# Token rows fetched ahead into the weight-staging pool, transposed tiles requested a step earlier, and seven attention output tiles, in a hybrid attention and linear-attention step

## The chip, the cores and the metric

The kernel runs on one core of a Trainium2 chip. The core has a matrix engine (PE, with its weight loads shown apart as PEld), a vector engine (DVE), an activation engine (ACT), a general engine (POOL), and a sequencer (SP) that in this kernel issues every DMA. Sixteen DMA engines carry the transfers. Each engine works through its own queue in order and waits there for semaphores. The metric is the device time of one execution in microseconds; lower is better.

## What is computed

One step of a one-layer decoder: 2048 prompt tokens, and 8 sequences with 8 new tokens each ("sample"), model width 1024, all in float32 at the interface. Cut to what matters:

```python
h = rmsnorm(x, norm_w)
z = h @ w_in                                   # 1024 x 3600
q, k, v, qb, kb, vb, g_lr, gate_a, gate_b = jnp.split(z, split_points(), axis=-1)
q = rope(rmsnorm(heads(q, 8), q_norm_w), pos)
k = rope(rmsnorm(heads(k, 8), k_norm_w), pos)
o_a = attend(q, k, heads(v, 8))                # three dilated windows, mixed by their denominators
log_a = log_sigmoid(g_lr @ w_gate_up + b_gate) / 16
o_b, s_fin = gla_chunked(qb * 64**-0.5, kb, vb, log_a, s0)
o_b = rmsnorm(o_b, gla_norm_w)
mixed = concat([o_a * silu(gate_a), o_b * silu(gate_b)])
y = x + mixed @ w_out
```

The attention has three branches: (window, dilation) = (128, 1), (512, 4) and (2048, 16). In a branch with dilation d the tokens of one residue modulo d form a sequence of their own, and each query sees 129 keys of it at most. The branch results are combined per token and head with weights from their maxima and softmax denominators.

## The kernel before

**Numbers in two halves.** Every float32 operand of a large product is split into two float16 parts (high and low). A projection of 128 tokens is 24 matrix products: 8 blocks of 128 inputs, and high x high, high x low, low x high.

**Normalised tokens.** `fetch(t)` (L464) loads the row block of 128 tokens `x_t`; `prep(t)` (L474) normalises it: a square with a sum on ACT into the scratch tile `jk` (L487), a reciprocal root in six small steps on ACT and DVE, a scaled copy on ACT (L495) and a difference on DVE (L496) into the two halves `ht`, then one transposing DMA `ht` to `hl` (L499) and a store of `hl` (L503) for later stages. The first four row blocks use two tiles of another pool (tag `qq`); those from 4 on and the sample's share a single buffer, tag `x` of pool `xp`. `ht` has one buffer as well. `hl` has four.

**Weights.** `load_w` (L544) loads a block of `w_in` as eight raw pieces of 128 rows (L554) into the pool `wr`, which has eight buffers of 128 x 528 float32; it finds a scale and splits them into `w` (L603, L604). Three such blocks are held at a time.

**First stage.** `first(m)` (L1085 on) runs over groups of four token tiles. Group 0 projects v, q and k of tiles 0 to 3; behind each k projection tile t+4 is fetched and prepared. Groups 1 to 3 project v, q, k of each tile and prepare tile t+4 up to tile 15. The results go through DRAM: the two-part `qp_d`, `kp_d`, `vp_d`. Behind `first(m)` the attention units of branches 1 and 2 of group m are put in a queue, and are worked off in small steps (`pump`) during the projections of group m+1.

**Attention.** `attend` (L395) makes an item of four steps: `pre` loads; `qk` makes scores in a PSUM bank and, on DVE, adds the mask and finds the row limit (L416), then takes the exponential on ACT (L419), whose sums go to the output tile; `tr` transposes the probabilities on PE and splits them; `pv` multiplies with the values, and `post` joins the halves (`added`, L458) into the output tile and stores it (L847, L903). Several items are in flight: two score banks, three score tiles `s`, three probability tiles `pt`.
- Branches 1 and 2: a unit is four heads of one block of 128 queries, in two items of two heads. Its output tile `o` (4 heads x 66 columns) is one of four in pool `op`. The transposed queries `qq` of a group and half come by four transposing DMAs (L801) in `queries`, are then exchanged between the partition halves by two DVE copies (`exchanged`, L794), and have two buffers.
- Branch 3: 16 residues with all eight heads, in two items (even heads, odd heads). Transposed queries and keys `T_q` and `T_k` (L883), two buffers each, the exchange (L794) right behind them, values `v` (L890), and one output tile of eight heads with two buffers, stored after the second item (L903).

**Beside and behind it.** During groups 2 and 3 and branch 3, POOL and DVE form the sample's dot products with the cached keys (L928, L929), whose loads are the most numerous DMAs. The projections qkb, g and vb run beside branch 3. Then come the linear attention (beside the rest of g, vb and gb), the combination of the branches and the output projection (L1431).

**Order.** The program is traced in the order of the code; a scheduler then orders each engine's instructions with a time model of its own. An instruction may stand far from its place in the code, as far as its data and its buffers allow, but the order on each queue is fixed once the kernel is compiled.

Of the kernel before, what the change touches and what calls it, by code (L numbers as in the profile page):

```python
# [18 lines left out]
P = 128  # L19
D = 1024  # L20
# [32 lines left out]
def tile_hymba(ctx: ExitStack, tc: tile.TileContext, A: dict):  # L53
# [292 lines left out]
    with ExitStack() as c1:  # L346
# [12 lines left out]

        wr = right(c_in, "wr", 8)  # L360
        zp = right(c_in, "zp", 2)
# [6 lines left out]
        ptp = c_att.enter_context(tc.tile_pool(name="ptp", bufs=3))  # L368
        op = c_att.enter_context(tc.tile_pool(name="op", bufs=4))
        ap_ = c_att.enter_context(tc.tile_pool(name="ap", bufs=2))  # L370
# [93 lines left out]
        def fetch(t):  # L464
            n = NS if t == "s" else P
            if t in (0, 1, 2, 3):
                if t % 2 == 0:
                    early.append(ap_.tile([P, 2, D], F32, name=f"x_{t}", tag="qq"))
                x = xs[t] = early[-1][:, t % 2]
            else:  # L470
                x = xs[t] = xp.tile([P, D], F32, name=f"x_{t}", tag="x", bufs=1)
            SP.dma_start(x[:n], x_s if t == "s" else x_p[t * P : (t + 1) * P, :])

        def prep(t):  # L474
            again[0] += 1
            n = NS if t == "s" else P
            u = again[0]
            x = xs.pop(t)[:]
            if t == "s":
# [7 lines left out]
            ACT.activation(jk[:n], x[:n], AF.Square, accum_out=ss[:n])  # L487
            rs = sm.tile([P, 1], F32, name=f"rs_{u}", tag="rs")
            rsqrt(sm, rs[:n], ss[:n], 1.0 / D, n, 1, f"x{u}", H_SCALE)
            if t != "s":  # L490
                if t < 4:
                    ht = early_ht[:, t]
                else:
                    ht = xp.tile([P, 2, D], F16, name=f"ht_{u}", tag="ht", bufs=1)[:]
                ACT.activation(ht[:, 0], x, AF.Copy, scale=rs[:])  # L495
                DVE.scalar_tensor_tensor(  # L496
                    ht[:, 1], x, rs[:], ht[:, 0], ALU.mult, ALU.subtract
                )
# [45 lines left out]
        def load_w(name, between=(), behind=()):  # L544
# [7 lines left out]
            for k in range(KT):  # L552
                raw = wr.tile([P, 528], F32, name=f"wr_{name}_{k}", tag="wr")
                SP.dma_start(raw[:, :n], src[k * P : (k + 1) * P, c0 : c0 + n])  # L554
# [241 lines left out]
        def queries(m, pp):  # L796

            q = qs_[m, pp] = ap_.tile([P, 2, 4, 512], F16, name=f"qq_{m}_{pp}", tag="qq")
            for a in range(4):
# [3 lines left out]
                )  # L803
            exchanged(*(q[:, a].rearrange("p h c -> p (h c)") for a in (1, 0)))

        def unit(m, pp, br, x):
# [13 lines left out]
            def pre():  # L820
                if (br, x) == (1, 0):
                    if pp == 0:
                        for a in range(4):
                            keys(m, a)
                        yield
                    queries(m, pp)
                    yield
# [47 lines left out]


        def branch3(r):
            T = {}

            def pre():  # L880
                for nm_, src, nb in (("q", qp_d, 16), ("k", kp_d, 8)):
                    t = b3.tile([P, nb, P], F16, name=f"T3_{nm_}_{r}", tag=f"T{nm_}")
                    SP.dma_start_transpose(t[:, 0:8], by16(src, r))  # L883
                    T[nm_] = t
                exchanged(
                    *(T["q"][:, a : a + 8].rearrange("p h i -> p (h i)") for a in (8, 0))
                )
                yield
                T["v"] = b3.tile([P, 1024], F16, name=f"v3_{r}", tag="v3")
                SP.dma_start(T["v"][:], by16(vp_d[:], r))  # L890
                T["o"] = b3.tile([P, NH, 66], F32, name=f"o3_{r}", tag="o3")

# [5 lines left out]
            def post(a):  # L898
                added(
                    T["o"][:].rearrange("p (i a) d -> p i a d", a=2)[:, :, a, 0:64], T["O", a][:]  # L900
                )
                if a:
                    SP.dma_start(by16(o3_d[:], r), T["o"][:].rearrange("p h d -> p (h d)"))  # L903

# [3 lines left out]
                    lambda i, a=a: [  # L908
                        (T["q"][:, 8 * part + 2 * i + a], T["k"][:, 2 * i + a])
                        for part in range(2)  # L910
                    ],
                    m3,
                    lambda i, b, a=a: T["v"][:, (2 * i + a) * P : (2 * i + a + 1) * P],
                    lambda i, a=a: T["o"][:, 2 * i + a, 65:66],
                    lambda i, a=a: T["o"][:, 2 * i + a, 64:65],
                    lambda i, a=a: OT(a, i),
# [914 lines left out]
```

## Time and profile before

| What | Value |
|---|---|
| Three runs | 1472.43, 1477.07, 1477.95 us; median 1477.07 |
| Profiled execution | 1483.62 us, span 1481.8 us |
| PE, share of the span | 1272.1 us, 86% |
| DVE | 1007.6 us, 68% |
| ACT | 855.7 us, 58% |
| POOL | 623.7 us, 42% |
| Granted TensorE clock, mean | 0.949 |

"Busy" is the time in which an engine executes; matrix products overlap, so a busy PE is not a PE at its peak. A row of waits names an engine and line that stood idle, who released it, and the total, the count and the longest. "DMA a<-b" is a transfer, from its issue to its landing. "SPq" is SP issuing or waiting. A chain of waits follows the last instruction back to what released each step.

By stage, in time: the first projections of group 0 (to about 95 us), the rest of them and the start of group 1 (to 170), groups 1 to 3 with branches 1 and 2 (to 676), branch 3 (to 853), linear attention (to about 1190), output.

### The profile page before, as it was taken

The numbers are of one execution on the slowest core, as the hardware profiler recorded it, in microseconds if no ns is written. First come the engines' busy times: TensorE is split into PE (matmuls) and PEld (weight loads), VectorE is DVE, ScalarE is ACT, GpSimd is POOL, SyncE is SP. The second block draws the span as 40 slices with busy tenths as digits, with TensorE's granted clock in tenths as the row PEclk, the third lists the DMA queues.
The fourth block names the chain that finished last, engine by engine and source line by source line (L and its number), as shares of the span: only waits on it lengthen the run. The fifth ranks groups of instructions, "written<-read, shape, count | busy, mean of one in ns | idle before, by whom it ended". The sixth has DMA issues, their size and how long they took to land.

```text
span 1481.8 us, 26480 instructions
## 1 busy us (share of the span) xinstructions
PE 1272.1 (86%) x8878; PEld 738.0 (50%) x8878; DVE 1007.6 (68%) x2444; ACT 855.7 (58%) x2295; POOL 623.7 (42%) x565
## 2 busy tenths in 40 slices
PE   3884997888888778887689999898988979989997
PEld 1332554555555545555457756566655535444343
DVE  6384878788887846766756535798988598783222
ACT  6443686676657756766667844687786553231110
POOL 0051424566656535554431167555553155541000
PEclk9897999999999989999799999999999989999999
DMA  9765665678756599878877553343234569998662
GB/s 277 217 168 173 178 193 138 167 213 212 205 153 173 148 229 265 285 203 220 217 186 177 150 152 101 83 137 124 92 102 158 177 239 337 361 304 287 221 204 73
DMA packets 254810, 285.36 MB, mean 193 GB/s; under 512 B 125825, under 2 KB 156626, under 8 KB 254674
## 3 DMA queue, kind: packets, MB, share of 16 engines
q1 hardware_dynamic: 254674, 283.67, 65.3%
q8 instruction: 70, 1.15, 0.3%
q14 instruction: 66, 0.54, 0.1%
HBM read 183.19 MB, written 75.24 MB: 174 GB/s over the span
## 4 chain that ended last, share of the span: by engine, by line
PE 26%; DVE 26%; DMA 25%; ACT 11%; issue 6%; POOL 3%; SPq 3%; DVEq 0%; POOLq 0%; ACTq 0%
PE Y L1431 7%; DMA qb<-q_d 4%; DMA o_d<-o 4%; PE acc_vb L1065 3%; PE OS L1680 3%; DVE p L416 3%; ACT p L419 2%; DMA T_q<-qp_d 2%; PE acc_g L1065 2%; DMA x<-in_x_prompt 2%; DMA k<-in_cache_k_win 2%; POOL pr L928 2%; DVE qbd L220 1%; DVE sck L929 1%; ACT E L209 1%
## 5 line engine op out<-in xcount | busy, mean ns | idle before, releaser
L928 POOL TENSOR_TENSOR pr<-k,qb 128x512 f32<-128x512 f32 x128 | 172.3, 1346 | 205.9 <-DVE sck L929 121.5
L1065 PEld LDWEIGHTS <-hr 128*128 128x128 f16 x1824 | 178.1, 100 | 142.5 <-issue 27.6
L419 ACT ACTIVATE p<-p,o 128x256 f32<-128x256 f32 (+1 forms) x384 | 173.1, 453 | 129.2 <-DVE o L416 110.2
L1065 PEld LDWEIGHTS <-hl 128*128 128x128 f16 x1248 | 124.0, 101 | 178.4 <-issue 52.0
L1431 PE MATMUL Y<-w_o,mh 128*128 128x512 f16 x768 | 181.5, 383 | 8.4 <-ACT mh L1397 5.0
L441 PE MATMUL O<-v,pt 128*128 128x128 f16 x1200 | 119.0, 225 | 48.5 <-POOL pt L393 18.1
L393 POOL TENSOR_TENSOR pt<-p,pt 128x512 f16<-128x512 f32 (+1 forms) x80 | 92.8, 1159 | 147.6 <-ACT pt L392 126.7
L426 PE MATMUL t<-ident,p 128*128 128x128 f32 x600 | 121.1, 296 | 18.1 <-ACT p L419 16.2
L929 DVE TENSOR_REDUCE sck<-pr 128x8 f32<-128x512 f32 x128 | 87.2, 681 | 58.7 <-POOL pr L928 58.5
L441 PEld LDWEIGHTS <-pt 128*128 128x128 f16 x1200 | 86.1, 101 | 79.8 <-POOL pt L393 24.5
L1431 PEld LDWEIGHTS <-mh 128*128 128x128 f16 x768 | 72.1, 98 | 102.9 <-issue 23.2
L1065 PE MATMUL acc_v<-w_v,hl 128*128 128x512 f16 x384 | 96.6, 400 | 25.6 <-ACT zs_q L648 11.0
L416 DVE CUSTOM_DVE_ANT_0 p<-s,m3w,scl_s 128x128 f32<-128x128 f32 (+1 forms) x256 | 88.6, 395 | 30.3 <-DMA o_d<-o 26.5
L408 PE MATMUL s<-kk,qq 128*128 128x256 f16 (+1 forms) x512 | 81.6, 277 | 26.4 <-DVE o L416 25.1
L1065 PE MATMUL acc_g<-w_g,hr 128*128 128x272 f16 (+1 forms) x768 | 103.2, 283 | 1.0 <-ACT vbs L722 1.0
L1065 PE MATMUL acc_q<-w_q,hl 128*128 128x512 f16 x384 | 95.5, 395 | 6.5 <-DVE vp L735 6.5
L1065 PE MATMUL acc_vb<-w_vb,hr 128*128 128x512 f16 x384 | 94.1, 392 | 2.8 <-DVE so_g L622 2.8
L1065 PE MATMUL acc_k<-w_k,hl 128*128 128x512 f16 x384 | 92.0, 383 | 3.9 <-ACT zs_k L648 3.4
L426 PEld LDWEIGHTS t<-ident,p 128*128 128x128 f32 x600 | 74.3, 149 | 40.2 <-ACT p L419 29.2
L1397 ACT ACTIVATE mh<-tm 128x1024 f16<-128x1024 f16 x32 | 31.7, 1020 | 104.9 <-PE tm L1396 98.6
L1065 PE MATMUL acc_gb<-w_gb,hr 128*128 128x512 f16 x384 | 89.8, 388 | 2.1 <-DVE so_gb L622 2.1
L209 ACT ACTIVATE E<-D_e 128x256 f32<-128x256 f32 (+1 forms) x168 | 67.9, 412 | 27.6 <-DVE ks L216 19.1
(526 smaller groups left out, 2685.5 us busy)
## 6 DMA issues: line engine op xcount, KB each, us to landing
k<-in_cache_k_win SPq DMA_DIRECT2D x104, 256.0 KB
sv<-in_cache_v_win SPq DMA_DIRECT2D x104, 256.0 KB
hr<-h_d SPq DMA_DIRECT2D x44, 512.0 KB
qb<-q_d SPq DMA_DIRECT2D x64, 256.0 KB
oc<-o_d SPq DMA_DIRECT2D x48, 264.0 KB
o_d<-o SPq DMA_DIRECT2D x64, 132.0 KB
x<-in_x_prompt SPq DMA_DIRECT2D x16, 512.0 KB
h_d<-hl SPq DMA_DIRECT2D x16, 512.0 KB
```

The costliest lines, as they stand in the source:

```text
L209: ACT.activation(E[rows, i, :n], D[rows, half], AF.Exp, scale=1.0 / 16.0)
L393: POOL.tensor_tensor(l, f, h, ALU.subtract)
L408: PE.matmul(s_ps[:, i * w : (i + 1) * w], q, k, start=(n == 0), stop=(n == len(prods) - 1),)
L416: DVE.tensor_tensor_reduce(s[:, sl], s_ps[:, sl], mask, neg, BIG, ALU.add, ALU.min, nmf(i))
L419: ACT.activation(s[:, sl], s[:, sl], AF.Exp, bias=nmf(i), scale=-1.0, accum_out=denf(i))
L426: PE.transpose(p_ps[:, i * P : (i + 1) * P], t["s"][:, i * P : (i + 1) * P], ident[:])
L441: PE.matmul(o_, t["pt"][:, c, (i * nb + b) * P : (i * nb + b + 1) * P], vf(i, b), start=(n == 0), stop=(n == 2 * nb - 1),)
L928: POOL.tensor_tensor(pr[:], kt, qt, ALU.mult)
L929: DVE.tensor_reduce(out, pr[:].rearrange("p (u k d) -> p u k d", u=2, k=4), AX.X, ALU.add)
L1065: PE.matmul(z, a_[:, k, :], w[:, p_, k, cols], start=(k == 0 and i == 0), stop=(k == KT - 1 and i == 2),)
L1431: PE.matmul(Y[:], a_[:, k, :], w_[:, part, k, :512], start=(i == 0), stop=(i == len(prods) - 1),)
L1680: PE.matmul(OS[32 * x : 32 * x + 32, 0:256], ps(x), vs_[bb][:, 256 * u : 256 * u + 256], start=(i == 0), stop=(i == 13),)
```

## The change

Token rows from tile 4 on move out of their single buffer into the raw-weight pool, whose buffers become four pairs of raw pieces; a row block takes one pair, each of its halves 512 of 528 columns. `load_w("k")` is followed by fetches of tiles 4, 5 and 6; behind the k projection of tile t, and in groups 1 and 2, the fetch is that of tile t+7 (preparation stays at t+4). The sample's rows use the `ht` buffer. The transposed queries of a group's first half are requested at the end of `first(m)`, those of the second half in the unit (branch 2, residue 1) of the first half; the exchange is made where a half's units begin. In branch 3 the T tiles of residue r+1 are requested ahead of residue r's exchange; the heads of an item are 4a to 4a+3 instead of every second one; and each item has an output tile of its own from the pool `op`, which now has seven, with a store of its own.

```diff
-        wr = right(c_in, "wr", 8)
+        wr = right(c_in, "wr", 4)
-        op = c_att.enter_context(tc.tile_pool(name="op", bufs=4))
+        op = c_att.enter_context(tc.tile_pool(name="op", bufs=7))
...
+            elif t == "s":
+                x = xs[t] = xp.tile([P, D], F32, name=f"x_{t}", tag="ht", bufs=1)
             else:
-                x = xs[t] = xp.tile([P, D], F32, name=f"x_{t}", tag="x", bufs=1)
+                x = wr.tile([P, 2, 528], F32, name=f"x_{t}", tag="wr")[:, :, :512]
+                xs[t] = x
+                SP.dma_start(x, x_p[t * P : (t + 1) * P, :].rearrange("p (a c) -> p a c", a=2))
+                return
...
-                raw = wr.tile([P, 528], F32, name=f"wr_{name}_{k}", tag="wr")
+                if k % 2 == 0:
+                    pair = wr.tile([P, 2, 528], F32, name=f"wr_{name}_{k}", tag="wr")
+                raw = pair[:, k % 2]
...
-            exchanged(*(q[:, a].rearrange("p h c -> p (h c)") for a in (1, 0)))
...
-                    queries(m, pp)
+                    q = qs_[m, pp]
+                    exchanged(*(q[:, a].rearrange("p h c -> p (h c)") for a in (1, 0)))
+                    yield
+                elif (pp, br, x) == (0, 2, 1):
+                    queries(m, 1)
                     yield
...
+        def turned3(r):
+            for nm_, src, nb in (("q", qp_d, 16), ("k", kp_d, 8)):
+                t = b3.tile([P, nb, P], F16, name=f"T3_{nm_}_{r}", tag=f"T{nm_}")
+                SP.dma_start_transpose(t[:, 0:8], by16(src, r))
+                T3[r][nm_] = t
...
             def pre():
-                for nm_, src, nb in (("q", qp_d, 16), ("k", kp_d, 8)):
-                    t = b3.tile([P, nb, P], F16, name=f"T3_{nm_}_{r}", tag=f"T{nm_}")
-                    SP.dma_start_transpose(t[:, 0:8], by16(src, r))
-                    T[nm_] = t
+                if r == 0:
+                    turned3(0)
+                if r < 15:
+                    turned3(r + 1)
+                yield
                 exchanged(
                     *(T["q"][:, a : a + 8].rearrange("p h i -> p (h i)") for a in (8, 0))
                 )
-                yield
...
-                T["o"] = b3.tile([P, NH, 66], F32, name=f"o3_{r}", tag="o3")
+                for a in range(2):
+                    T["o", a] = op.tile([P, 4, 66], F32, name=f"o3_{r}_{a}", tag="o")
...
             def post(a):
-                added(
-                    T["o"][:].rearrange("p (i a) d -> p i a d", a=2)[:, :, a, 0:64], T["O", a][:]
-                )
-                if a:
-                    SP.dma_start(by16(o3_d[:], r), T["o"][:].rearrange("p h d -> p (h d)"))
+                o = T["o", a]
+                added(o[:, :, 0:64], T["O", a][:])
+                SP.dma_start(
+                    by16(o3_d[:, 264 * a : 264 * a + 264], r), o[:].rearrange("p h d -> p (h d)")
+                )
...
-                                at_once(load_w("k"))
+                                at_once(load_w("k", (), [4, 5, 6]))
                         elif name == "k":
-                            fetch(t + 4)
+                            fetch(t + 7)
                             prep(t + 4)
...
+                if t < 9:
+                    fetch(t + 7)
                 if t < 12:
-                    fetch(t + 4)
                     prep(t + 4)
...
+            queries(m, 0)
             for pp in range(2):
```

More of the change, by code (lines that the diff above doesn't have):

```diff
@@ L478, in prep @@
             x = xs.pop(t)[:]
+            wide = t != "s" and t > 3
+            as_x = lambda ap: ap.rearrange("p (a c) -> p a c", a=2) if wide else ap
             if t == "s":
@@ L486, in prep @@
             jk = zp.tile([P, D], BF16, name=f"jk_{u}", tag="z1")
-            ACT.activation(jk[:n], x[:n], AF.Square, accum_out=ss[:n])
+            ACT.activation(as_x(jk[:n]), x[:n], AF.Square, accum_out=ss[:n])
             rs = sm.tile([P, 1], F32, name=f"rs_{u}", tag="rs")
@@ L494, in prep @@
                     ht = xp.tile([P, 2, D], F16, name=f"ht_{u}", tag="ht", bufs=1)[:]
-                ACT.activation(ht[:, 0], x, AF.Copy, scale=rs[:])
+                ACT.activation(as_x(ht[:, 0]), x, AF.Copy, scale=rs[:])
                 DVE.scalar_tensor_tensor(
-                    ht[:, 1], x, rs[:], ht[:, 0], ALU.mult, ALU.subtract
+                    as_x(ht[:, 1]), x, rs[:], as_x(ht[:, 0]), ALU.mult, ALU.subtract
                 )
@@ L874, in unit @@
             return out
+        T3 = [{} for _ in range(16)]
+        def turned3(r):
[3 more added lines that the diff above has]
+                T3[r][nm_] = t
         def branch3(r):
-            T = {}
+            T = T3[r]
             def pre():
-                for nm_, src, nb in (("q", qp_d, 16), ("k", kp_d, 8)):
-                    t = b3.tile([P, nb, P], F16, name=f"T3_{nm_}_{r}", tag=f"T{nm_}")
-                    SP.dma_start_transpose(t[:, 0:8], by16(src, r))
-                    T[nm_] = t
+                if r == 0:
[3 more added lines that the diff above has]
+                yield
                 exchanged(
@@ L908, in branch3 @@
                     lambda i, a=a: [
-                        (T["q"][:, 8 * part + 2 * i + a], T["k"][:, 2 * i + a])
+                        (T["q"][:, 8 * part + 4 * a + i], T["k"][:, 4 * a + i])
                         for part in range(2)
@@ L912, in branch3 @@
                     m3,
-                    lambda i, b, a=a: T["v"][:, (2 * i + a) * P : (2 * i + a + 1) * P],
-                    lambda i, a=a: T["o"][:, 2 * i + a, 65:66],
-                    lambda i, a=a: T["o"][:, 2 * i + a, 64:65],
+                    lambda i, b, a=a: T["v"][:, (4 * a + i) * P : (4 * a + i + 1) * P],
+                    lambda i, a=a: T["o", a][:, i, 65:66],
+                    lambda i, a=a: T["o", a][:, i, 64:65],
                     lambda i, a=a: OT(a, i),
```

## The prediction

> **What bounds the kernel now.** I read the page first (span, shares, the chain that ended last), then the stretches between the stages, then who waits for whom inside each stretch, and last the timelines of single engines. The stretches, one row each (length, then busy microseconds of PE, PEld, DVE, ACT and POOL, the granted TensorE clock, the DMA share, GB/s):
>
> ```profile
> span 1481.8 us, 26480 instructions
> ...
> 95.00:170.00 75.00, 52.02 (x230) 23.15 (x229) 47.89 (x93) 32.97 (x77) 22.30 (x23) 0.86 0.61 171
> 170.00:380.00 210.00, 184.53 (x1296) 114.55 (x1295) 170.19 (x424) 152.94 (x444) 114.21 (x87) 0.96 0.66 181
> 380.00:540.00 160.00, 130.21 (x879) 81.48 (x877) 126.66 (x284) 102.71 (x284) 89.37 (x67) 0.91 0.70 182
> 540.00:676.00 136.00, 119.54 (x831) 72.54 (x830) 85.37 (x225) 89.82 (x251) 75.15 (x61) 0.96 0.85 248
> 676.00:853.00 177.00, 146.29 (x1236) 106.31 (x1234) 112.63 (x428) 125.31 (x437) 54.41 (x50) 0.91 0.73 185
> 853.00:1190.00 337.00, 308.43 (x2415) 193.22 (x2414) 247.60 (x523) 227.30 (x582) 179.45 (x202) 0.98 0.42 128
> 1190.00:1482.00 292.00, 266.65 (x1738) 118.94 (x1736) 161.62 (x334) 69.19 (x109) 73.83 (x57) 0.97 0.74 252
> ```
>
> Length less PE busy is PE idle: 23.0 us in 95 to 170 (the last projections of token group 0, then group 1), 25.5, 29.8 and 16.5 in the three stretches of attention branches 1 and 2, 30.7 in branch 3 (676 to 853), 28.6 and 25.4 behind it. PE is the fullest engine in each of these rows, and the matrix products of later stages already fill gaps (the gate projections run beside branch 3). So a removed wait is worth only what PE idle it removes; the rest comes back as PE work done later. The change touches only the stretches up to 853.
>
> Three kinds of wait belong to the edits. All of the program, then 95 to 170, 380 to 540 and 676 to 853 (microseconds in total, times, longest):
>
> ```profile
> DVE p L416 <- DMA o_d<-o: 29.8, 17, 6.0
> DVE T_q L794 <- DMA T_q<-qp_d: 29.6, 12, 7.2
> ACT jk L487 <- DMA x<-in_x_prompt: 19.1, 7, 6.7
> ...
> ACT jk L487 <- DMA x<-in_x_prompt: 14.1, 4, 6.7
> PE acc_v L1065 <- ACT zs_q L648: 11.0, 1, 11.0
> PE acc_v L1065 <- ACT zs_k L648: 6.6, 1, 6.6
> ...
> PE s L408 <- DVE o L416: 17.1, 8, 6.2
> DVE p L416 <- DMA o_d<-o: 11.6, 5, 6.0
> ...
> DVE T_q L794 <- DMA T_q<-qp_d: 27.3, 11, 7.2
> DVE p L416 <- DMA o_d<-o: 11.6, 9, 3.0
> ```
>
> **Rows of x.** There is one x buffer for tiles from 4 on. The chain in time order (start, length, what):
>
> ```profile
> 108.87 4.63 DMA x<-in_x_prompt
> 113.52 1.15 ACT jk L487 x2
> 114.67 0.58 ACT sq_k L647
> ...
> 124.19 5.21 DMA x<-in_x_prompt
> 129.41 1.15 ACT jk L487 x2
> ...
> 158.75 4.67 DMA x<-in_x_prompt
> 163.44 1.15 ACT jk L487 x2
> ```
>
> A load leaves when the tile before it has been normalised, takes 4.6 to 5.2 us, and the square (jk) stands at the head of ACT until it lands. The eviction of a finished k or q projection is queued behind it on ACT, and PE stands for lack of a free accumulator: the 11.0 and 6.6 us above. With four paired slots in the raw-weight pool and loads three tiles ahead, these three DMA pieces leave the chain: 4.63 + 5.21 + 4.67 = 14.5 us. All of it is on the path (the attention of group 0 cannot start before), and it fits into the 17.6 us for which PE stands. The loads after 170 us are worth the 2 us or so that ACT still waits for them under a fuller PE; I put nothing.
>
> Tile 4 loses: its row was fetched early into the free buffer, and now has to wait for a pair of k-weight raws.
>
> ```profile
> 29.04 0.38 SPq L472 DMA_DIRECT2D x<-in_x_prompt  x1
> ...
> 84.36 1.47 SPq L554 DMA_DIRECT2D wr_qkb<-in_w_in  x2
> ...
> 94.84 1.05 ACT L487 ACTIVATE jk<-x 128x1024 bf16<-128x1024 f32 x1
> ```
>
> 84.36 is when the first raw slot is free in this trace (the qkb raws take it). A pair frees one raw later, about 85.5; with 5.2 us to land the row is there at about 90.7, 4 us before its use. Costed at nothing; if that cover fails it costs the excess. The qkb raws that lose these slots load once the rows are used up; their first reader belongs to the end of group 3. Pairs also free one raw later in the start-up: at most 1 us.
>
> **Seven output tiles.** In branches 1 and 2 the masked scores (p) write their denominators into an output tile, one of four, free only when the store of four units earlier has landed. DVE stood 11.6 us for that in 380 to 540, and PE's 17.1 us for a scores bank is the same stall handed on. Three score tiles and three probability tiles allow at most six items (pairs of heads) between p and the value product, some four units; seven tiles cover them and the store. I take the direct DVE wait of the three stretches: 29.8 less 11.6 in branch 3, 18.2 us. From 380 to 540 all of it reaches PE (17.1 behind 11.6), in the other two PE has projections to go on with, so I take 60%: 11 us. Bounds: nothing, and the 18.2.
>
> In branch 3 an output tile held a whole residue, two buffers, and was stored after the second half.
>
> ```profile
> 814.50 0.85 DVE L794 COPY T_q<-T_q 64x1024 f16<-64x1024 f16 x2 [2.77 <-DMA T_q<-qp_d]
> 815.54 0.35 DVE L416 CUSTOM_DVE_ANT_0 p<-s,m3w,scl_s 128x128 f32<-128x128 f32 x1 [0.18 <-DMA o_d<-o]
> ...
> 831.65 0.35 DVE L416 CUSTOM_DVE_ANT_0 p<-s,m3w,scl_s 128x128 f32<-128x128 f32 x1 [2.11 <-DMA o_d<-o]
> ...
> 810.02 1.24 SPq L883 DMA_TRANSPOSE T_q<-qp_d  x1
> 811.76 1.22 SPq L903 DMA_DIRECT2D o_d<-o  x1
> ...
> 828.83 0.55 SPq L903 DMA_DIRECT2D o_d<-o  x1
> ```
>
> The store at 811.76 releases p at 815.54, the store at 828.83 releases p at 831.65: these are residues 12 and 14, so two residues take 16.1 us, and the loop through the output tile sets the pace. With seven halves the same loop spans three and a half residues and stops deciding. What is next is ACT, 125.31 us busy in the 177: the stage cannot end more than 52 us sooner, and no more than its 30.7 us of PE idle can be won. Since the wait for T (next) stays, I take a little under half of that idle: 14 us. Bounds 0 and 30.7. A second store per residue adds 16 issues, off the path while seven buffers cover them.
>
> The Trainium skill, page "DMA: Bandwidth & Descriptors", section "Rules for kernel authors", speaks against splitting: many small transfers should be joined, and its section on the anatomy of one DMA fits about 2.0 us fixed to each. By that, 16 more stores would be an estimated 32 us if each stood on the path, and would nearly eat the whole gain. The trace agrees that size hardly matters (a store of the whole tile landed 3.8 us after its issue at 811.76), but such a store stands on the path here only while a buffer is short.
>
> **Transposed queries and T tiles asked for earlier.** The order in the program is not the order on a queue: a load goes out once its buffer is free. T_q at 810.02 is residue 14's, asked for two residues before its use, and SP itself waits there for a matmul, the last reader of that buffer:
>
> ```profile
> SPq L883 <- PE t L426: 4.3, 4, 1.6
> ...
>   DMA qq<-qp_d: 3.8, 3
> ...
> L408 PE MATMUL s<-kk,qq x512: 216/273/421, 159.1 to 675.9; 128*128 128x256 f16 x144, 128*128 128x128 f16 x27
> ```
>
> There are still two T buffers, so asking earlier moves nothing: 0 us. What DVE loses (2.77 us in the row at 814.50) comes from the copy being placed too soon behind its DMA, 17 us ahead of its own p. The change puts one more step ahead of the copy in the program, which may let that order drift either way: bounds minus 17 us (the PE idle of branch 3 not yet used) and plus 27 (the wait of 27.3 doubled); I take the wait as it stands, 0. On SP a T load that waits holds the value loads and stores behind it, by the 4.3 us that it already holds them. For the queries the wait is 3.8 us in three places; 0. The copies are as many and as long as before.
>
> **Sum.** 14.5 + 11 + 14 = 39.5, less 1.5 for pairs and the issues that show: 38 us. The profiled execution took 1483.62 us (span 1481.8), 0.4% over the median of the three runs, 1477.07. From the median: **1439 us**.
>
> **Rivals.**
>
> The forecast, 48%: about 1439.
>
> The T wait goes too, 15%: if the copies land behind their data, branch 3 loses the other 17 us of idle: 1477 - 38 - 17 = 1422. For it speaks that 27.3 us of DVE time stand there; against it the unchanged buffers. The Trainium skill, same page and section, says that a DMA issued early and awaited late hides its fixed cost; by that rule this case would be the result. The trace shows the early issue already in place, held by the buffer.
>
> Only the rows count, 18%: score and probability tiles (three each) or the T loop take the place of the output tile at once, so that p waits as long for something else: 1477 - 14.5 = 1462. For it: the three-deep tiles are the next ring, and T stalls DVE as much as the output tile.
>
> What is freed is given back, 12%: the stages shift, but the gates' products that now lie in the gaps follow behind, at PE 92% busy from 853 on (308.43 of 337). Then within 7.4 us of 1477, which is the 0.5% that a measurement of this kernel can tell from no change.
>
> A new wait on ACT, slower, 7%: with x at hand, the scaled copy into ht (one buffer) goes to ACT directly behind the square and stands there until the transposing DMA of the tile before has landed.
>
> ```profile
> 38.52 5.14 DMA hl<-early_ht
> ...
> L499 SPq DMA_TRANSPOSE hl<-ht x12: 1851/2026/3495, 105.8 to 382.8; - x12
> ```
>
> At 5.14 us for each of 12 tiles it costs 62 us: 1477 - 38 + 62 = 1501. It outweighs the gain from 38 / 12 = 3.2 us per tile, and reads slower from 3.8. Against it: the 12 transposes spread over 277 us, 25 us apart on average, and only the first four come close together.
>
> **How the numbers follow.** Faster by over 0.5% is the forecast, the T case and the rows-only case: 0.48 + 0.15 + 0.18 = 0.81. Same 0.12, slower 0.07. The range goes from 1412 (the T case with 10 us more out of the 18.2 and 30.7 us bounds) to 1474 (half of the given-back case); outside lie the slower case, the other half and a tail below, together about 0.18.
>
> **What would show it.** Right: no ACT wait for x behind tile 0, and the first scores product well before 159.1 us; DVE p no longer waiting for o_d in either part; two residues of branch 3 in under 14 us instead of 16.1, with ACT fuller there; T_q waits still in the twenties. PE idle ahead of the end of branch 3 down by about 38 us. Wrong: p waits as long for POOL, ACT or a bank; ACT's ht waiting for hl; PE idle moved behind 853; or the T waits gone.

## Result and profile after

| | before | after |
|---|---|---|
| Median of the runs taken together | 1477.51 us (1472.43 to 1478.08, 4 runs) | 1430.53 us (1425.19 to 1433.19, 4 runs) |
| Profiled execution | 1483.62 us | 1425.19 us |
| Its span | 1481.8 us | 1423.4 us |
| Granted TensorE clock, mean | 0.949 | 0.963 |

The ratio is 0.9685, 95% interval 0.9649 to 0.9720: 47 us faster. The two profiled executions lie 58 us apart, because the one of before is slow for its median and the one of after is the fastest of its four. So 58 is explained below where traces are compared, and 47 where times are.

The stretches of the kernel before, this time cut where its stages begin (the first 95 us, up to the first scores product, branches 1 and 2, branch 3 up to its last scores product, the linear attention up to its last state update, the output). Columns as in the prediction: length, busy microseconds of PE, PEld, DVE, ACT and POOL, the granted clock, the DMA share, GB/s.

```profile
0.00:95.00 95.00, 64.49 (x267) 27.79 (x268) 55.60 (x137) 55.43 (x119) 14.98 (x22) 0.93 0.79 233
95.00:159.10 64.10, 41.12 (x166) 17.16 (x165) 41.91 (x69) 24.43 (x50) 22.30 (x23) 0.84 0.59 158
159.10:676.00 516.90, 445.17 (x3065) 274.57 (x3064) 388.20 (x957) 354.00 (x1002) 278.74 (x214) 0.95 0.73 201
676.00:835.30 159.30, 128.65 (x1098) 94.15 (x1096) 104.21 (x395) 112.13 (x395) 49.00 (x40) 0.90 0.77 193
835.30:1160.50 325.20, 296.74 (x2413) 191.12 (x2414) 239.13 (x505) 223.91 (x583) 177.30 (x205) 0.98 0.40 120
1160.50:1481.80 321.30, 295.98 (x1879) 133.20 (x1877) 178.52 (x383) 85.75 (x151) 81.40 (x63) 0.97 0.73 248
```

The same stages of the kernel after:

```profile
0.00:95.00 95.00, 66.89 (x283) 29.16 (x284) 56.91 (x149) 58.53 (x127) 17.14 (x25) 0.98 0.76 231
95.00:141.10 46.10, 37.86 (x174) 16.80 (x173) 37.16 (x65) 25.39 (x51) 22.96 (x20) 1.00 1.00 246
141.10:618.80 477.70, 419.92 (x2984) 265.02 (x2983) 384.94 (x944) 345.43 (x986) 275.81 (x209) 0.96 0.76 207
618.80:755.90 137.10, 111.87 (x967) 81.55 (x965) 105.85 (x392) 104.58 (x378) 55.14 (x45) 0.90 0.96 225
755.90:1063.40 307.50, 284.99 (x2431) 191.60 (x2429) 226.17 (x476) 213.47 (x568) 174.75 (x200) 0.98 0.38 116
1063.40:1423.40 360.00, 331.65 (x2048) 150.51 (x2047) 191.08 (x421) 106.25 (x190) 86.09 (x70) 0.96 0.72 241
```

Length less PE busy gives PE's idle time. It reads, before and after: 30.5 and 28.1, 23.0 and 8.2, 71.7 and 57.8, 30.7 and 25.2, 28.5 and 22.5, 25.3 and 28.4. The sum falls from 209.7 to 170.2, by 39.5 us; up to the end of branch 3 it falls by 36.6. The other 18.9 us of the 58 are PE busy time (1272.1 to 1253.2), for the same 8878 matrix products. Busy time multiplied by the mean granted clock (0.949 and 0.963) is 1207 in both, so the higher clock is large enough to account for those 18.9 us. That is a sum and no proof: with the rows alone the clock rose from 0.949 to 0.956 and PE busy did not fall (1273.4).

The row of branch 3 is easily misread. It is 22.2 us shorter, but PE idle fell by only 5.4: 131 products fewer lie in it (967 against 1098), and the output stage has 169 more and is 38.7 us longer.

The waits of the kernel after over all of the program (who waits for whom, microseconds in total, times, longest), to be set beside those of the prediction:

```profile
DVE T_q L803 <- DMA T_q<-qp_d: 20.9, 9, 4.6
...
ACT ht L502 <- DMA hl<-ht: 5.1, 3, 2.2
...
DVE p L416 <- DMA o_d<-o: 4.7, 3, 2.0
...
PE acc_q L1086 <- ACT zs_k L657: 3.9, 1, 3.9
...
ACT jk L494 <- DMA x<-in_x_prompt: 2.6, 1, 2.6
```

The wait for rows fell from 19.1 to 2.6, and what is left is that of the first row block at the start (2.9 before): behind it ACT waits for no row of the prompt. PE's waits of 11.0 and 6.6 fell to one of 3.9, the wait of p for the store from 29.8 to 4.7. The wait for T_q stands at 20.9 (29.6 before).

In branch 3, the store issues on SP show the pace (start, length). Before, there is one for each residue; of the sixteen the first, the seventh and the fifteenth:

```profile
701.03 0.41 SPq L903 DMA_DIRECT2D o_d<-o  x1
...
775.45 0.53 SPq L903 DMA_DIRECT2D o_d<-o  x1
...
847.17 0.38 SPq L903 DMA_DIRECT2D o_d<-o  x1
```

After, there are two for each residue, so every fourth is two residues later. Shown are the 9th, 13th, 17th, 19th, 21st and 23rd of 32:

```profile
690.04 0.33 SPq L922 DMA_DIRECT2D o_d<-o  x1
...
708.32 0.32 SPq L922 DMA_DIRECT2D o_d<-o  x1
...
725.54 1.04 SPq L922 DMA_DIRECT2D o_d<-o  x1
...
734.31 0.38 SPq L922 DMA_DIRECT2D o_d<-o  x1
...
741.61 0.32 SPq L922 DMA_DIRECT2D o_d<-o  x1
...
747.94 0.32 SPq L922 DMA_DIRECT2D o_d<-o  x1
```

Before, two residues took 24.8 us on average in the first six (701.03 to 775.45) and 17.9 in the next eight; the 16.1 us of the prediction is one of its fastest places. After, they take 23.3 in the first four (the first store is issued at 643.42), then 18.3, 17.2 and 16.1, and 13.6 from 734.31 on. From the first store to the last, two residues take 16.5 us against 20.3. So the stage has a slow part in both kernels. In the slowest two residues after (659.5 to 690.0) DVE is busy 27.6 of 30.5 us, with the sample's dot products beside the scores; that these set the pace there is a reading of one trace and was not tried.

### The profile page after: what moved, and what is told of

It reads as the page before. It is cut to its first block, busy times and chain, and to the rows that moved or that the text cites. A ratio compares the mean times of both kernels' runs of the same rounds, so it can differ in the third digit from the quotient of the medians.

```text
span 1423.4 us, 26539 instructions
## 1 busy us (share of the span) xinstructions
PE 1253.2 (88%) x8878; PEld 734.6 (52%) x8878; DVE 1002.1 (70%) x2444; ACT 853.7 (60%) x2295; POOL 631.9 (44%) x565
## 4 chain that ended last, share of the span: by engine, by line
PE 24%; DVE 16%; DMA 13%; ACT 4%; POOL 4%; issue 3%; SPq 1%; DVEq 0%; POOLq 0%; ACTq 0%
PE Y L1454 11%; PE OS L1703 3%; DVE qbd L220 2%; DMA T_q<-qp_d 2%; DMA qb<-q_d 2%; DMA k<-in_cache_k_win 2%; POOL pr L949 2%; PE acc_vb L1086 1%; PE acc_g L1086 1%; PE acc_gb L1086 1%; ACT E L209 1%; DVE p L416 1%; DVE Ac_e L250 1%; DVE ks L216 1%; DMA hr<-h_d 1%
## 5 line engine op out<-in xcount | busy, mean ns | idle before, releaser
L441 PE MATMUL O<-v,pt 128*128 128x128 f16 x1200 | 113.4, 227 | 32.7 <-POOL pt L393 9.4
L426 PE MATMUL t<-ident,p 128*128 128x128 f32 x600 | 110.8, 288 | 10.2 <-ACT p L419 4.7
L408 PE MATMUL s<-kk,qq 128*128 128x256 f16 (+1 forms) x512 | 82.4, 273 | 18.9 <-DVE o L416 16.3
L1086 PE MATMUL acc_v<-w_v,hl 128*128 128x512 f16 x384 | 91.4, 383 | 7.9 <-DVE vp L744 2.7
L426 PEld LDWEIGHTS t<-ident,p 128*128 128x128 f32 x600 | 70.9, 147 | 22.4 <-ACT p L419 10.9
```

The source lines that it names most:

```text
L408: PE.matmul(s_ps[:, i * w : (i + 1) * w], q, k, start=(n == 0), stop=(n == len(prods) - 1),)
L426: PE.transpose(p_ps[:, i * P : (i + 1) * P], t["s"][:, i * P : (i + 1) * P], ident[:])
L441: PE.matmul(o_, t["pt"][:, c, (i * nb + b) * P : (i * nb + b + 1) * P], vf(i, b), start=(n == 0), stop=(n == 2 * nb - 1),)
L1086: PE.matmul(z, a_[:, k, :], w[:, p_, k, cols], start=(k == 0 and i == 0), stop=(k == KT - 1 and i == 2),)
```

## Experiments

Each ratio is against the kernel before, run beside it on the same chip; microseconds saved are one less the ratio, of 1478.

| Kernel | median, us | ratio | 95% interval | saved, us |
|---|---|---|---|---|
| before + rows | 1447.8 | 0.9792 | 0.9761 to 0.9823 | 31 |
| before + output tiles (six) | 1448.4 | 0.9802 | 0.9766 to 0.9838 | 29 |
| before + requests | 1460.3 | 0.9876 | 0.9847 to 0.9905 | 18 |
| after, rows fetched near | 1437.8 | 0.9717 | 0.9688 to 0.9746 | 42 |
| before + empty step | 1461.0 | 0.9884 | 0.9855 to 0.9913 | 17 |
| before, credit 0.5 | 1478.7 | 1.0003 | 0.9985 to 1.0022 | 0 |
| after, four T tiles | 1431.7 | 0.9680 | 0.9648 to 0.9712 | 47 |
| after, T_q apart | 1432.3 | 0.9684 | 0.9658 to 0.9710 | 47 |
| after less the step | 1445.3 | 0.9777 | 0.9753 to 0.9801 | 33 |
| before + requests less the step | 1452.9 | 0.9839 | 0.9815 to 0.9864 | 24 |
| rows + seven output tiles | 1439.8 | 0.9745 | 0.9720 to 0.9769 | 38 |
| the same + empty step | 1427.6 | 0.9649 | 0.9618 to 0.9679 | 52 |

**The three parts, each alone on the kernel before.** Rows:

```diff
-        wr = right(c_in, "wr", 8)
+        wr = right(c_in, "wr", 4)
...
+                x = wr.tile([P, 2, 528], F32, name=f"x_{t}", tag="wr")[:, :, :512]
...
-                            fetch(t + 4)
+                            fetch(t + 7)
...
```

> The kernel before with the rows alone: raw weights in four pairs, token rows from tile 4 on in the same pool, fetched three tiles ahead; four output tiles and the requests as before. My theory (rows worth 14.5 us, less 1 for the pairs): no ACT wait for x behind tile 0, the first scores product near 141 us instead of 159, and about 1463 us (1456 to 1468). Rival (the start's gain is given back in the later stages unless the output tiles follow): the first product near 141 us all the same, but 1471 us or more. Rival (the rows carry nearly everything): 1445 us or less.

Output tiles. There are six, since seven do not fit into the memory beside the old buffer of x:

```diff
-        op = c_att.enter_context(tc.tile_pool(name="op", bufs=4))
+        op = c_att.enter_context(tc.tile_pool(name="op", bufs=6))
...
-                T["o"] = b3.tile([P, NH, 66], F32, name=f"o3_{r}", tag="o3")
+                for a in range(2):
+                    T["o", a] = op.tile([P, 4, 66], F32, name=f"o3_{r}_{a}", tag="o")
...
```

> The kernel before with the output tiles alone, and six of them instead of seven (seven do not fit beside the old x buffer): branch 3 writes halves into the same pool and stores each. My theory (11 + 14 us by the prediction): DVE p's wait for o_d falls below 8 us, branch 3 (first to last scores product) shortens from 159 us by 15 or more, and about 1452 us (1445 to 1460). Rival (score and probability tiles or the T loop take over at once): p's wait is gone but branch 3 lasts within 5 us of before and the time is 1470 or more.

Requests, with the further step that the change brings along:

```diff
...
-                    queries(m, pp)
+                    q = qs_[m, pp]
+                    exchanged(*(q[:, a].rearrange("p h c -> p (h c)") for a in (1, 0)))
                     yield
+                elif (pp, br, x) == (0, 2, 1):
+                    queries(m, 1)
+                    yield
...
+                if r < 15:
+                    turned3(r + 1)
+                yield
                 exchanged(
...
+            queries(m, 0)
```

> The kernel before with the earlier requests alone: queries of the first half at the end of the group's projections, of the second half some steps ahead, T tiles one residue ahead, the exchanges at use; one x buffer, four output tiles, whole residues stored. My theory: nothing, 1477 us within 7, with the T wait of DVE still at 20 us or more, as the T buffers are as many and the loads already stood where a buffer came free. Rival (the copies now land behind their data): T wait under 8 us and 1463 us or less.

They saved 31, 29 and 18 us: 78 in sum, where all three together save 47. For the output tiles that is as expected (1448.4, in 1445 to 1460). The rows came out far better than expected (1447.8, not 1456 to 1468), and so did the requests (1460.3, not 1477). Where each acts is seen by the scores products of branches 1 and 2 (the count, then ns, then first and last start). Rows alone:

```profile
L408 PE MATMUL s<-kk,qq x512: 216/272/422, 141.0 to 636.1; 128*128 128x256 f16 x144, 128*128 128x128 f16 x27
```

Output tiles alone:

```profile
L408 PE MATMUL s<-kk,qq x512: 216/272/422, 156.6 to 642.9; 128*128 128x256 f16 x144, 128*128 128x128 f16 x27
```

With rows alone the first product starts 18.1 us earlier than the 159.1 of before, as early as in the kernel after: the start belongs to the rows. Output tiles leave it at 156.6 and shorten what follows (486 us from first to last against 517). In PE's idle time by stage, worked out as above:

| Stage | before | rows | outputs | rows + seven outputs | the same + step | after |
|---|---|---|---|---|---|---|
| first 95 us | 30.5 | 27.5 | 31.3 | 29.6 | 29.2 | 28.1 |
| to the first scores | 23.0 | 7.4 | 22.3 | 8.2 | 7.9 | 8.2 |
| branches 1 and 2 | 71.7 | 64.2 | 53.9 | 54.2 | 54.4 | 57.8 |
| branch 3 | 30.7 | 27.5 | 23.4 | 29.2 | 24.7 | 25.2 |
| linear attention | 28.5 | 21.7 | 26.2 | 28.0 | 24.4 | 22.5 |
| output | 25.3 | 22.9 | 31.9 | 27.5 | 31.0 | 28.4 |
| PE busy | 1272.1 | 1273.4 | 1265.2 | 1265.0 | 1254.6 | 1253.2 |

Rows alone save 15.6 us before the first scores, and 12.4 us in branch 3 and behind. The second amount is gone when the output tiles are added (branch 3 and behind: 84.5 before, 72.1 with rows, 84.7 with both). In branches 1 and 2, rows and outputs save 7.5 and 17.8 us alone, and 17.5 together. These two places hold most of what is missing between 31 + 29 and 38. What the rows did in the late stages, where they have nothing to do, was not found out.

So the price of a part depends on what it is measured on. The rows are worth 31 us on the kernel before; the output tiles add only 7 to them (31 to 38, with intervals that overlap a little: 0.9761 to 0.9823 and 0.9720 to 0.9769).

**Distance or buffers.** The kernel after, with rows fetched right ahead of their preparation:

```diff
-                                at_once(load_w("k", (), [4, 5, 6]))
+                                at_once(load_w("k"))
...
-                            fetch(t + 7)
+                            fetch(t + 4)
...
```

> The changed kernel with the distance taken back: rows still in the four pairs, but each fetched in the program directly ahead of its own preparation (tile t+4 where t+7 was). My theory (a load goes out when its buffer is free, whatever its place in the program, so it is the buffers that count): no ACT wait for x behind tile 0, first scores product within 3 us of 141, and the changed kernel's time within 7 us, about 1430. Rival (the distance in the program counts): the ACT waits for x come back, some 14 us between 95 and 170 us, and about 1445 us.

The waits for rows stay away (the one that is left is the first row block's), the first scores product comes at 143.5, and 42 us are saved against 47, with intervals that overlap:

```profile
ACT jk L494 <- DMA x<-in_x_prompt: 2.3, 1, 2.3
```

The rival's 14 us of waits do not come back, so the buffers carry the gain. The distance adds some 5 us, not told apart from nothing.

**Is the requests' 18 us the order?** I had put them at 0. Two kernels leave the work, the buffers and the loads of before as they are and change only the order. One has an empty step where the change has its further one:

```diff
+                elif (pp, br, x) == (0, 2, 1):
+                    yield
```

> The kernel before with one empty step more in the unit (branch 2, residue 1) of a group's first half: no work, buffer or load changes, only the order that the program's scheduler finds. Theory A (the 18 us of the earlier requests are a re-roll of an order that was unlucky): this kernel too moves by more than 0.5%, 5 to 20 us below 1477, with the T_q waits at 25 to 35 us as before. Theory B (the requests are worth 18 us by themselves): within 7 us of 1477, ratio 0.995 to 1.005.

The other shifts all attention steps by half a step:

```diff
-        credit = rate = 0.0
+        credit, rate = 0.5, 0.0
```

> The kernel before with the pump's starting credit at 0.5 instead of 0, which shifts by half a step where attention steps fall among the projections: the same work, buffers and loads. Theory A (order is worth 10 to 20 us by itself): off by more than 7 us, likelier below 1477 than above. Theory B (only the edits' own mechanisms count): within 7 us of 1477.

The empty step alone saves 17 us, as much as the requests with it, though the wait for T_q, expected at 25 to 35 us, is 13.0. The half step moves nothing. So not every change of order helps: this one does. The table has what was saved with and without the step:

| Surroundings | without the step | with it | the step's worth |
|---|---|---|---|
| before | 0 | 17 | 17 |
| before + requests | 24 | 18 | -6 |
| rows + seven outputs | 38 | 52 | 14 |
| the change (rows, outputs, requests) | 33 | 47 | 14 |

The lower three rows rest on these kernels. The change without the step, and the requests alone without it:

```diff
                 elif (pp, br, x) == (0, 2, 1):
                     queries(m, 1)
-                    yield
```

> The kernel after without the one extra step that the change adds in the unit (branch 2, residue 1); the second half's queries are still requested there. Theory A (of the requests' 18 us alone, the extra step made all; it parts the items and so eases a stall that seven output tiles ease too): without it the kernel after stays within 7 us of 1430, as the stall is gone anyway. Theory B (the step is worth its 17 us in any surroundings): 1440 to 1450.

> The kernel before with the earlier requests alone, without the extra step. If the step made the gain of the requests: within 7 us of 1477 (ratio 0.995 to 1.005). If the earlier requests themselves made it: 1455 to 1465 again.

Rows and seven output tiles without anything of the requests, and then with the step as an empty one:

```diff
...
-                    q = qs_[m, pp]
-                    exchanged(*(q[:, a].rearrange("p h c -> p (h c)") for a in (1, 0)))
+                    queries(m, pp)
                     yield
-                elif (pp, br, x) == (0, 2, 1):
-                    queries(m, 1)
-                    yield
...
```

> The kernel after with nothing of the requests: rows and seven output tiles alone, no extra step. If rows and outputs add up (31 and 29 us alone): 1415 to 1425, and the requests cost time within the change. If the requests are worth nothing within the change: within 7 us of 1430. If they are worth their 18 us there: 1440 to 1450.

```diff
+                elif (pp, br, x) == (0, 2, 1):
+                    yield
```

> Rows and seven output tiles with the extra step as an empty one, queries and T tiles requested as before. Theory A: the same as the kernel after within 7 us, 1423 to 1437, since only the requests' places differ. If the requests' places matter by themselves: off by more than 7 us, and the difference to the kernel after is their worth.

Rows and seven output tiles come to 1439.8, where I had expected 1430 if the requests were worth nothing: what is missing is the step, since with it they reach 1427.6. Both theories that I had of the requests fall. The step does not make their gain on the kernel before (they save 24 without it, and the -6 of the table is not told apart from nothing, as the intervals overlap; what the requests do there was not followed), and on the change it is not idle either (14 us, with intervals that don't touch: 0.9753 to 0.9801 without, 0.9649 to 0.9720 with). The requests themselves read 5 us worse in both pairs within the change (38 to 33, 52 to 47), with intervals that overlap in both. So within the change they are worth nothing that was measured. Rows, seven output tiles and an empty step (52) are the best kernel measured, not told apart from the change itself.

**Where the step's gain lies.** Not at one place. What each stage is shorter with the step, in the three pairs of traces, cut as above (the two traces of a pair lie further apart than the medians, as their executions lie differently about them):

| Stage | before, with the empty step | rows + seven outputs, with the empty step | the change, with its step |
|---|---|---|---|
| up to the first scores | 1.7 | -1.6 | 3.2 |
| branches 1 and 2 | 18.1 | -1.1 | 0.8 |
| branch 3 | 1.4 | 6.9 | -4.6 |
| linear attention | 15.4 | 6.7 | 15.1 |
| output | -12.6 | 4.7 | 6.5 |
| span | 24.0 | 15.6 | 21.0 |

On the kernel before, 18.1 us lie in branches 1 and 2, where the step is; of the 15.4 in the linear attention the output gives 12.6 back. Within the change next to nothing is won there. The gain lies further back, in the linear attention (6.7 and 15.1) and the output, and in one of the two pairs in branch 3. The linear attention of the change without the step, to be read against its row in the second fence above:

```profile
755.30:1077.90 322.60, 294.17 (x2458) 197.62 (x2457) 233.25 (x489) 214.99 (x572) 171.01 (x199) 0.95 0.36 108
```

Branch 3 ends at the same time (755.3 and 755.9), and the linear attention takes 322.6 us instead of 307.5: 15.1 of the 21.0 us between these two traces. Of the 15.1, 5.9 are PE idle (28.4 against 22.5). The other 9.2 are busy time, at a clock of 0.95 instead of 0.98 and with 27 products more. One place of it, in four short windows:

```profile
820.00:832.00 12.00, 11.69 (x95) 7.30 (x93) 7.86 (x12) 4.74 (x12) 5.73 (x5) 1.00 0.35 99
832.00:837.00 5.00, 0.33 (x1) 0.29 (x2) 0.89 (x3) 0.75 (x2) 2.61 (x3) 0.80 0.68 157
837.00:842.00 5.00, 5.00 (x13) 2.70 (x12) 0.00 (x0) 0.00 (x0) 0.00 (x0) 0.51 0.00 0
842.00:847.00 5.00, 5.00 (x31) 2.62 (x29) 3.23 (x3) 1.01 (x2) 3.88 (x2) 1.00 0.17 56
```

PE stands from 832 to 837, then runs 13 products in 5 us at a clock of 0.51. What it stood for, and what came next, show in the group of these products in the linear attention (count, busy us, mean ns, idle time before them and its cause). Without the step:

```profile
L1309 PE MATMUL O_s<-S,qxs 128*64 128x256 f32 x32 | 10.0, 478 | 5.0 <-DMA S<-in_state_gla 5.0
```

With it, in the kernel after:

```profile
L1310 PE MATMUL O_s<-S,qxs 128*64 128x256 f32 x32 | 7.5, 381 | 2.3 <-DMA S<-in_state_gla 2.3
```

The wait is for the load of the sample's states. It is 2.7 us longer without the step, and the 32 products then take 10.0 us instead of 7.5: 5.2 us of the 15.1 at this one place. The rest is spread over the stage and wasn't followed. Rows and seven output tiles without the step have the same wait, 5.1 us, and with the empty step 0.2. The kernel before has none without the step and 0.4 with it, so this load has no part in the step's 17 us there. That the step moved the load is read from the traces; no kernel moved the load alone, and how one empty step reaches this far stays open.

**The wait for T_q.** The prediction put it down to the copy being placed too soon behind its DMA, with the buffers holding the request. Four T tiles in flight:

```diff
+            both = None
+            if r % 4 > 1:
+                both = ap_.tile([P, 32, P], F16, name=f"T3_{r}", tag="qq")
...
+                    t = both[:, 0:16] if nm_ == "q" else both[:, 16:24]
```

> The kernel after with four T tiles of queries and keys in flight in branch 3 instead of two (every second pair of residues uses the two tiles that hold branch 1 and 2's queries earlier on). If the wait for T_q is held by the buffer, as the prediction says: it falls from 20.9 us to under 8, branch 3 (137 us to its last scores) gets up to 15 us shorter, 1415 to 1425. If it comes from the copy standing close behind its DMA in the compiled order: the T_q wait stays at 15 to 25 us and the time within 7 us of 1430.

The loaded half in a tile of its own, three deep, with six output tiles for the room:

```diff
-                t = b3.tile([P, nb, P], F16, name=f"T3_{nm_}_{r}", tag=f"T{nm_}")
+                t = b3.tile([P, 8, P], F16, name=f"T3_{nm_}_{r}", tag=f"T{nm_}", bufs=nb)
...
+                T["x"] = b3.tile([P, 8, P], F16, name=f"T3_x_{r}", tag="Tx")
+                exchanged(*(T[n_][:].rearrange("p h i -> p (h i)") for n_ in "xq"))
```

> The kernel after with the loaded half of T_q in a tile of its own with three buffers, the exchanged half in another with two, and six output tiles instead of seven for the room: loads no longer wait for the products that read the exchanged half. Buffer theory: T_q waits under 8 us, branch 3 up to 15 us shorter, 1415 to 1425. Placement theory: T_q waits 15 to 25 us, time within 7 us of 1430.

The waits of the two kernels, four T tiles first (the tiles of the added pair are named T):

```profile
DVE T L803 <- DMA T<-qp_d: 11.2, 4, 3.8
...
DVE p L416 <- DMA o_d<-o: 7.5, 8, 1.6
...
DVE T_q L803 <- DMA T_q<-qp_d: 5.2, 3, 2.5
```

```profile
DVE p L416 <- DMA o_d<-o: 17.9, 9, 4.9
...
DVE T_x L803 <- DMA T_q<-qp_d: 5.8, 4, 3.2
```

With four tiles the two waits come to 16.4 us, hardly less than 20.9, as the theory of the copy's place has it. With three-deep loads the wait falls to 5.8, and the wait of p for a store rises from 4.7 to 17.9. The time stays in both (1431.7 and 1432.3 against 1430.5). So more room for T was worth nothing in either form; in the second the stall came back at the output tile, of which there is one fewer there.

Three kernels that leave the T buffers and the place of the T loads in the program as they were say more. Their waits for T_q, with the output tiles alone, the empty step alone, and the rows alone:

```profile
DVE T_q L794 <- DMA T_q<-qp_d: 10.6, 5, 3.8
```

```profile
DVE T_q L794 <- DMA T_q<-qp_d: 13.0, 10, 3.4
```

```profile
DVE T_q L803 <- DMA T_q<-qp_d: 32.1, 13, 3.8
```

With the same two buffers the wait lies anywhere from 10.6 to 32.1 us, so the buffers alone do not set it. And the time does not follow it: these kernels save 29, 17 and 31 us.

## Why the prediction was right, and where it was not

The forecast was 1439 and the likeliest case; 1430.5 lies within its range, 9 us below.

Two lines of the kernel before, in time (start, length, and in brackets the engine's idle time before them and its cause), bear on the first term:

```profile
145.79 1.06 ACT L487 ACTIVATE jk<-x 128x1024 bf16<-128x1024 f32 x1 [6.67 <-DMA x<-in_x_prompt]
...
148.15 2.29 PE L1065 MATMUL acc_v<-w_v,hl 128*128 128x512 f16 x5 [11.04 <-ACT zs_q L648]
```

Term by term:

- **Rows, 14.5 us: the mechanism right, the sum in part luck.** PE idle before the first scores product fell by 14.8, the product came 18.0 us earlier, and ACT waits for no row of the prompt behind the first. Row 4's later load did no harm. But the three pieces that the prediction adds up are not what was saved. The third (158.75 to 163.4) lies at and behind the first scores product at 159.14, where PE is busy throughout. In its place belongs the load of the two lines above, for which ACT stood 6.67 us and, behind it, PE 11.04; it is not in the sum. PE's own waits say it better: 11.0 and 6.6 us before, against one of 3.9 after. On the kernel before, the rows alone save 31 us, twice the price, and what they save behind branches 1 and 2 is not explained.
- **Output tiles in branches 1 and 2, 11 us: right in kind.** PE idle there fell by 17.8 with the six tiles alone (71.7 to 53.9), and by 10.0 when seven tiles are added to the rows (64.2 to 54.2); in the kernel after it is 13.9 below the kernel before.
- **Output tiles in branch 3, 14 us: mis-sized, 5.4 measured.** With six tiles alone it is 7.3, and on top of the rows nothing (27.5 to 29.2). The stage did get 22 us shorter. But its gaps had held products of the later projections, which then had to be run afterwards: the very thing that the prediction had said of gaps in general and did not charge here. "Two residues in under 14 us" came true only near the end of the stage (13.6), though ACT is fuller there, as forecast (104.6 of 137.1 us against 112.1 of 159.3). The output tile was one limit among others. The DMA share of this stage is now 0.96, against 0.77; whether that is the next limit wasn't tried.
- **The sum, 38 us: partly luck.** PE idle up to the end of branch 3 fell by 36.6, and rows with seven output tiles alone, the two parts to which the prediction gave a price, saved 38. But the parts measured one by one do not have their prices. The rows save 31 us, not 14.5, and the outputs add 7 to them, not 25. The errors cancel.
- **Requests and T tiles, 0 us: not refuted within the change, wrong on the kernel before, and wrong for what came with them.** Within the change the requests measured 0 to 5 us to the bad, and the wait for T is 20.9. On the kernel before, without the step, they save 24. And the change's further step in the unit (branch 2, residue 1) was not costed at all. With it the compiled order is another, and it is worth 14 us within the change. That is the term that the prediction lacks: 38, less the requests' 5 (with intervals that overlap), and 14 for the step make the 47.
- **The clock, no term.** The sum took PE's work as fixed. In all fourteen traces PE busy by granted clock is 1204 to 1217 us, so time is roughly idle time plus some 1210 over the clock: from 0.949 to 0.963 that is an estimated 18.5 us of the 58 between the profiled executions. The spread of 13 us among the traces is almost as large. The clock differs between executions of one kernel too (0.953 to 0.963 in the four of the kernel after), which is part of why 58 is more than 47.

The rivals. "The T wait goes too": fell; the wait stayed, and taking most of it away by three-deep loads won nothing there, with one output tile fewer. "Only the rows count": fell by its mechanism, as p no longer waits so long for something else; yet the rows alone save 31 of the 38 us that rows and outputs save, where this rival gave them 14.5. "What is freed is given back": true of branch 3 alone. "A new wait on ACT": its mechanism is there (no such wait before), at three waits and 5.1 us instead of 62. The Trainium skill, page "DMA: Bandwidth & Descriptors", speaks against small transfers: the 16 further stores show no price in the waits, as p waits 4.7 us for stores in all. The 2.0 us behind the recorded 32 are that page's fit for DMAs issued from GpSimd, and here SP issues them all.

## What to carry to other kernels

Price a freed stall by the idle time of the bounding engine and then ask what work had lain in that stall's gaps: it comes back later. Where a compiler orders the queues, a change's empty or added steps are a part of it with a price of their own; put a neutral step into the kernel before as a control, and measure the parts within the change and not only alone, since 31 + 29 + 18 made 47. A sum that comes out right does not show that its terms are. In this trace a long idle gap of PE cost its length and then slow products behind it (5.0 us and 2.5 more).

## What the hardware showed beyond that

A PE wait of 5.0 us was followed by 5 us at a granted clock of 0.51, which raised the mean of the products there from 381 to 478 ns, and by full clock after that. Cut into single microseconds, the clock reads 1.00 until 835, which is 3.3 us after the last product's end at 831.7, and 0.50 to 0.56 from there to 842; it is back at 1.00 some 5.2 us after the products began again at 836.7. The Trainium skill, page "TensorE: Matmul & The Clock Gate", Part 1, says that the clock falls to half after an idle window of about 3.4 us and comes back after a busy one of that length. The trace agrees with the fall; the return took longer here. A wait of 2.3 us in the same place left that mean at 381 ns, and a wait of 5.1 us (rows and seven output tiles) raised it only to 431, so the price of such a gap is not fixed. In the stretch from 95 us to the first scores product the granted clock is 0.81 to 0.86 in the traces that have PE's long waits (11 and 7 us), and 0.93 to 1.00 in those with the rows' own buffers.
